# Half-chunk products in column halves, scores that alternate heads, and earlier loads, in a four-mixer decoder layer

## The chip, the cores and the metric

The kernel runs on one core of one Trainium2 chip. Its time is what the device takes for one execution, in microseconds (us). TensorE (PE) multiplies matrices into PSUM banks; VectorE (DVE), ScalarE (ACT) and GpSimd (POOL) work on tiles; the queues of SyncE (SP), ScalarE and GpSimd issue the transfers (DMA). Every engine works through its own instructions in their order, and semaphores let one wait for another.

## The reference

One decoder layer on 1024 tokens of width 1024, all in float32 (`DEPTH` is 1):

```
x = x + 0.5 * swiglu_ffn(rms_norm(x, norm_ffn1), ffn1_w_in, ffn1_w_out)
x = x + token_mixer(rms_norm(x, norm_mix), w_in, w_out, ...)
x = x + 0.5 * swiglu_ffn(rms_norm(x, norm_ffn2), ffn2_w_in, ffn2_w_out)
return rms_norm(x, norm_final)
```

`swiglu_ffn` is `(silu(gate) * up) @ w_out` with `gate, up = split(x @ w_in)` of 2816 columns each. `token_mixer` projects its input and gives four groups of 256 channels to four causal mixers: a pooling over trailing windows; two gated linear attentions (HGRN2 and GLA), each with 4 heads of 64 channels and

```
S_t = diag(a_t) S_{t-1} + k_t^T v_t,    o_t = q_t S_t
```

and RWKV7, a delta rule with 4 heads of 64:

```
S_t = S_{t-1} diag(w_t) - (S_{t-1} kk_t)(kk_t * a_t)^T + v_t k_t^T,    o_t = S_t r_t
```

The four results are normalised, gated and joined, and `w_out` brings them back to 1024 channels.

## The kernel before

**Large products.** An activation or weight tile is split into a high and a low part of type fp32r (`split`, `wload`: ScalarE copies the high part, VectorE subtracts it for the low one), and a product is three fp32r products, high by high, high by low and low by high (`acc3`). Everything goes through the helper on line 89, so in the profile nearly all matmuls carry that line, and the tile names tell them apart. Small products are plain fp32; each leaves two records in the trace.

**The feed-forward blocks** work on pairs of 128-row blocks of the 2816 hidden rows, with seven block products in place of eight (`seven`, `out_seven`). One pair, number `PLAIN` = 0, goes through in the plain way: its four h tiles (two row blocks by two token halves) are written to DRAM (`put_h`, h1d and h2d), and after `out_seven` the four are loaded again, split, and multiplied with their two rows of the output weights. `out_seven` runs over five blocks of pairs, and over four quarters `q` of the output columns in each; in quarter `q` it fetches the weights of the next quarter (`wfetch`, tile wraw, two buffers), prepares those of this one in whi and wlo (four buffers each), and adds seven products into the tiles of x (gr, gg) with VectorE (L672) and GpSimd (L675). In the first block (`ffn1_out`) the plain pair's loop also adds to x (L747) and splits the result for the mixers (`norm_tile`, L177 to L181); its weights go through wraw, whi and wlo by `wload`. In the second (`ffn2_out`) the loop works on token-major tiles (`token_major`, L794, L796), and the final norm follows.

**The mixers** (`weave`) are one stream of large products (`dense_stream`) into which the steps of several generators are put: `rwkv` (delta rule), `gates` (the two attentions) and others. A generator yields a time from the table `LAT`; a clock that counts the estimated cost of each matmul decides when its next step is due, and the order of TensorE's instructions is fixed by it. The list that Tile schedules gives these steps priority over the dense stream.

**The attentions** (`attend`, called for two mixers, two channel pairs and two token halves, 8 times). A tile holds two heads by 512 tokens, in four columns of 128 tokens. The decays within a chunk of 128 are handled by seven levels of block size m = 1, 2, 4, 8, 16, 32, 64: at a level, the odd blocks' queries of both heads are put block-diagonally into `bdt`, k by `bdt` gives the scores of that level in a bank pg, and for m < 64 a mask copy (L1547, `copy_predicated`) puts the right ones into `PT`, whose entries hold scores of 128 keys by 128 queries per column and head. For m < 64 the keys and queries that count lie in the same half of 64 tokens; rows 64 to 127 by columns 0 to 63 of `PT` stay zero. At the end, for each of the four columns, one product of q with the state `Sb` and one product of `PT` with the values `Vp` per head go into the bank O.

**The delta rule** (`rwkv_unit`, 4 units of two heads by 8 chunks of 64). Its scores are 16 products, each of the 64 rows of one head (rows 0 to 63 or 64 to 127), into banks px of four chunks; VectorE multiplies each bank with two masks (L1293, L1294). The inverse and the chunk recurrence (banks py and po) follow.

## Time and profile before

| | us |
|---|---|
| median of 3 runs | 2066.91 |
| lowest, highest | 2062.92, 2071.9 |
| the profiled execution | 2059.14 |
| its span, first to last instruction | 2057.3 |
| PE busy in it | 1979.4 (96%) |
| DVE busy | 1541.1 (75%) |
| ACT busy | 964.2 (47%) |
| POOL busy | 442.0 (21%) |

The profile is of one execution. A row of the timeline gives the start and the length of a run of like instructions, the engine, the line, the operation, the tiles written and read, the tile shape for a matmul (rows by columns of the array, then partitions by columns of the moving operand), and in brackets the idle time before it and what ended that. Matmuls are pipelined, so lengths overlap, and starts are the safer reading. PEld is the load of the stationary operand, SPq a DMA issue of SyncE's queue. A row of the waits gives who waited for whom: us in total, times, longest. A row of the groups gives busy us, mean ns of one, and idle time before them.

### The profile page before, as it was taken

The page shows a single profiled execution, that of the slowest core. Times are in us where ns is not written, and L with a number is a line of the kernel's source. Part 1 is how long each engine was busy: PE and PEld are TensorE (multiplying, and loading weights), DVE is VectorE, ACT ScalarE, POOL GpSimd, SP SyncE. Part 2 cuts the span into 40 slices and gives each one's busy share as a digit, 9 for nine tenths or more (in the row PEclk, how much of TensorE's full clock was granted, in tenths as well). Part 3 has the DMA queues.
Part 4 walks back from the last instruction along what each step waited for, and adds up shares of the span by engine and source line. Part 5 has one row for each costly group of instructions (what it writes and reads, how often), then busy time and mean ns, then how long its engine had stood idle before and what let it go on. Part 6 is the DMA issues. An engine that isn't in the chain of part 4 may idle for free. (4 is left out here: it accounts for less than half of the span.)

```text
span 2057.3 us, 29356 instructions
## 1 busy us (share of the span) xinstructions
PE 1979.4 (96%) x10424; PEld 1594.1 (77%) x10424; DVE 1541.1 (75%) x2575; ACT 964.2 (47%) x1801; POOL 442.0 (21%) x449
## 2 busy tenths in 40 slices
PE   7899999999999899989999999999999999999995
PEld 5688888887887678778778787787888887778884
DVE  5868878768878856486576676676978898777786
ACT  7435444544443655343464543444544444444444
POOL 0011110003446602002020010100111222134464
PEclk9999999999999999999999999999999999999998
DMA  8336554457653453333443244655445666786622
GB/s 275 114 93 205 200 189 161 157 186 280 253 203 138 156 159 108 91 92 97 145 147 106 83 140 134 207 172 160 139 162 187 202 211 215 242 289 254 246 89 91
DMA packets 304402, 348.60 MB, mean 169 GB/s; under 512 B 28160, under 2 KB 230240, under 8 KB 304256
## 3 DMA queue, kind: packets, MB, share of 16 engines
q1 hardware_dynamic: 301152, 339.14, 49.8%
q0 software_dynamic: 1664, 4.95, 0.7%
q10 hardware_dynamic: 1440, 2.65, 0.4%
q8 instruction: 82, 1.34, 0.3%
q14 instruction: 64, 0.52, 0.1%
HBM read 234.22 MB, written 112.46 MB: 169 GB/s over the span
## 5 line engine op out<-in xcount | busy, mean ns | idle before, releaser
L89 PE MATMUL mm<-xs,whi 128*128 128x512 f32 x1568 | 521.0, 413 | 10.3 <-ACT xs L177 3.9
L89 PEld LDWEIGHTS mm<-xs,whi 128*128 128x128 f32 x1568 | 287.4, 192 | 81.5 <-issue 8.5
L89 PE MATMUL mm<-xs,wlo 128*128 128x512 f32 x784 | 315.4, 402 | 12.1 <-DVE wlo L146 9.7
L145 ACT CAST whi<-wraw 128x512 fp32r<-128x512 f32 (+1 forms) x192 | 118.1, 620 | 171.7 <-PE mm L89 121.1
L300 ACT CAST whi<-wsum 128x512 fp32r<-128x512 f32 x176 | 108.3, 620 | 179.2 <-PE pq L89 49.4
L89 PEld LDWEIGHTS mm<-xs,wlo 128*128 128x128 f32 x784 | 150.6, 192 | 50.4 <-DVE wlo L146 12.1
L89 PE MATMUL pq<-xs,whi 128*128 128x512 f32 x576 | 181.0, 394 | 2.3 <-ACT xs L177 1.8
L146 DVE TENSOR_TENSOR wlo<-wraw,whi 128x512 fp32r<-128x512 f32 (+1 forms) x192 | 134.3, 707 | 63.2 <-ACT whi L145 51.1
L89 PE MATMUL pg<-xs,whi 128*128 128x512 f32 x560 | 176.9, 395 | 4.7 <-DVE hx L559 2.7
L89 PE MATMUL px<-xs,whi 128*128 128x512 f32 x560 | 175.2, 393 | 1.2 <-DVE xs L178 1.2
L301 DVE TENSOR_TENSOR wlo<-wsum,whi 128x512 fp32r<-128x512 f32 x176 | 121.5, 697 | 28.2 <-ACT whi L300 27.9
L89 PE MATMUL pq<-xe,whi 128*128 128x512 f32 x448 | 139.2, 392 | 0.0
L89 PEld LDWEIGHTS pq<-xs,whi 128*128 128x128 f32 x576 | 108.5, 189 | 27.2 <-ACT xs L177 2.7
L89 PEld LDWEIGHTS pg<-xs,whi 128*128 128x128 f32 x560 | 105.0, 189 | 29.5 <-issue 3.1
L89 PEld LDWEIGHTS px<-xs,whi 128*128 128x128 f32 x560 | 105.2, 188 | 25.9 <-DVE xs L178 2.3
L89 PE MATMUL pq<-xs,wlo 128*128 128x512 f32 x288 | 114.2, 396 | 3.8 <-DVE wlo L301 3.8
L340 POOL TENSOR_TENSOR tmp<-tmp 128x512 f32<-128x512 f32 x22 | 33.1, 1503 | 374.0 <-ACT tmp L330 310.6
L89 PE MATMUL pg<-xs,wlo 128*128 128x512 f32 x280 | 110.3, 394 | 0.0
L89 PE MATMUL px<-xs,wlo 128*128 128x512 f32 x280 | 109.9, 392 | 0.0
L89 PEld LDWEIGHTS pq<-xe,whi 128*128 128x128 f32 x448 | 84.3, 188 | 18.7
L622 ACT CAST whi<-wsum 128x512 fp32r<-128x512 f32 x80 | 49.7, 621 | 95.1 <-PE px L89 25.5
L340 POOL TENSOR_TENSOR gr<-gr 128x512 f32<-128x512 f32 x18 | 36.6, 2031 | 256.7 <-ACT gr L330 198.0
(460 smaller groups left out, 4319.9 us busy)
## 6 DMA issues: line engine op xcount, KB each, us to landing
hs<-hx SPq DMA_DIRECT2D x126, 512.0 KB, 3.4
xs<-hs SPq DMA_DIRECT2D x90, 512.0 KB, 6.5
wraw<-in_ffn_w_in SPq DMA_DIRECT2D x68, 512.0 KB, 4.1
wraw<-in_w_in SPq DMA_DIRECT2D x52, 512.0 KB, 4.1
wrawb<-in_ffn_w_in SPq DMA_DIRECT2D x44, 512.0 KB, 4.6
wraw<-in_ffn_w_out SPq DMA_DIRECT2D x42, 512.0 KB, 3.6
xe<-hs SPq DMA_DIRECT2D x36, 512.0 KB, 7.4
wraw<-in_w_out SPq DMA_DIRECT2D x16, 512.0 KB, 4.1
```

The source lines that it names most:

```text
L89: return self._add(self.nc.tensor.matmul(out, lhsT=lhsT, rhs=rhs, **kw), n * 0.42e-3 if rhs.dtype == F32R else max(n * 1.68e-3, 0.04))
L145: nc.scalar.copy(hi[:, :n], raw[:, sl])
L146: nc.vector.tensor_tensor(lo[:, :n], raw[:, sl], hi[:, :n].bitcast(F32), op=ALU.subtract)
L300: nc.scalar.copy(hi[:, :H], a)
L301: nc.vector.tensor_tensor(lo[:, :H], a, hi[:, :H].bitcast(F32), op=ALU.subtract)
L340: nc.gpsimd.tensor_tensor(kept[5], kept[5], kept[7], op=ALU.add)
L622: nc.scalar.copy(v(hi), src)
```

## The change

There are three parts.

*Loads.* `out_seven` gets an argument `late`, a function that it calls in the last block when quarter q = 2 begins, after the fetch of quarter 3. In `ffn1_out` it loads and splits the plain pair's four h tiles and its four weight tiles, the latter through `tmp` into tiles hx and xe instead of wraw, whi and wlo. In `ffn2_out` it loads the final norm's gain and loads and splits the four h tiles; the weights stay where they were.

```
+                if last and q == 2:
+                    late()
...
+        def late():
+            hs.extend([[h_tile(f, h) for h in range(2)] for f in (f0, f0 + 1)])
+            for n in range(0, KT, 2):
+                raw = wk.tile([P, H], F32, name="tmp")
+                nc.sync.dma_start(raw.rearrange("p (f c) -> p f c", c=256), wo[:, f0:f0 + 2, n * P:(n + 2) * P])
+                if n < 6:
+                    t = wk.tile([P, 2 * H], F32R, name="hx", bufs=3)
+                else:
+                    t = wk.tile([P, 2 * H], F32R, name="xe", bufs=6)
+                hi, lo = self.split(raw, t=t)
+                w.append([(hi[:, f * 256:f * 256 + 256], lo[:, f * 256:f * 256 + 256]) for f in range(2)])
...
-        hs = [[h_tile(f, h) for h in range(2)] for f in (f0, f0 + 1)]
-        w = [self.wload([(wo[:, f0:f0 + 2, n * P:(n + 2) * P], 0, None)], 2, 256, 1) for n in range(0, KT, 2)]
...
+        def late():
+            gf = self.gf = wk.tile([P, D], F32, name="wrawb", bufs=2)
+            nc.scalar.dma_start(gf, self.A["norm_final"].broadcast_to([P, D]))
+            for f in (f0, f0 + 1):
+                hp.append([])
+                for h in range(2):
+                    t = tmp()
+                    nc.sync.dma_start(t, self.hd[f, h])
+                    hp[-1].append(self.split(t))
```

*Scores of the delta rule.* The same 16 products come in two halves of four chunks; in a half, the products of the two heads alternate and go into two banks. One yield of twice the time stands where two stood.

```
-        for c2 in range(4):
-            ps = self.px.tile([P, 4, P], F32, name="px")
-            hd = c2 // 2
-            hs = slice(hd * 64, hd * 64 + 64)
+        for half in range(2):
+            banks = [self.px.tile([P, 4, P], F32, name="px") for _ in range(2)]
             for i in range(4):
...
+                for hd, ps in enumerate(banks):
+                    hs = slice(hd * 64, hd * 64 + 64)
+                    te.matmul(ps[:, i], lhsT=bk[hs, 4 * half + i].rearrange("p x t -> p (x t)"),
+                              rhs=rK[hs, 4 * half + i].rearrange("p x t -> p (x t)"), start=True, stop=True)
...
-            if c2 in (1, 2):
-                yield LAT["score"]
+            if half == 0:
+                yield 2 * LAT["score"]
```

*The attentions.* At a level with m < 64 each half of 64 tokens has a product of its own (64 keys by 32 queries of each head), into the output partitions of its half; the mask copy becomes two of 64 partitions. The product of `PT` with the values becomes two: queries 0 to 63 with keys 0 to 63, and queries 64 to 127 with all 128 keys, each into the output partitions of its queries.

```
-                te.matmul(ps[:, j].rearrange("p x t -> p (x t)"), lhsT=k[:, j * P:(j + 1) * P],
-                          rhs=self.bdt[:, i % 2, j].rearrange("p x t -> p (x t)"), start=True, stop=True)
+                if m < 64:
+                    for u in range(2):
+                        te.matmul(ps[u * 64:u * 64 + 64, j, :, 0:32], lhsT=k[:, j * P + u * 64:j * P + u * 64 + 64],
+                                  rhs=self.bdt[:, i % 2, j, :, u * 32:u * 32 + 32], start=True, stop=True)
...
+                for u in range(2):
+                    us, n = slice(u * 64, u * 64 + 64), 32 // m
+                    dst = PT.rearrange("p j x (n y m) -> p (j x) n y m", y=2, m=m)[us, :, u * n:u * n + n, 1]
+                    msk = self.gmask[us, 64 * i + u * 32:64 * i + u * 32 + 32].rearrange("p (n m) -> p n m", m=m)
+                    nc.vector.copy_predicated(dst, msk.unsqueeze(1).broadcast_to([64, 8, n, m]), ...)
...
-                te.matmul(O[:, j, hs], lhsT=PT[:, j, hd], rhs=Vp[:, j, hs], start=False, stop=True,
-                          skip_group_check=True)
+                for u in range(2):
+                    r = slice(0, 64 * u + 64)
+                    te.matmul(O[u * 64:u * 64 + 64, j, hs], lhsT=PT[r, j, hd, u * 64:u * 64 + 64], rhs=Vp[r, j, hs],
+                              start=False, stop=True, skip_group_check=True)
```

## The prediction

> **What bounds the kernel now.** I read the page first: TensorE is busy for 96% of the span and VectorE for 75%, so whatever takes TensorE time out of the middle of the program should show one for one, and only where TensorE idles can another engine set the pace. The stretches of 50 us and the waits then say where it idles.

> ```profile
> span 2057.3 us, 29356 instructions
> PE 1979.4 (96%) x10424; PEld 1594.1 (77%) x10424; DVE 1541.1 (75%) x2575; ACT 964.2 (47%) x1801; POOL 442.0 (21%) x449
> ...
> 650.00:700.00 50.00, 38.67 (x159) 29.04 (x158) 48.68 (x58) 29.94 (x51) 36.67 (x25) 0.96 0.41 148
> ...
> PE mm L89 <- DVE wlo L146: 9.7, 4, 7.0
> ...
> PE pg L89 <- DVE PT L1547: 6.4, 1, 6.4
> ```

> The columns after the stretch are its length, then PE, PEld, DVE, ACT, POOL, clock, DMA share and GB/s. Two of the three things edited lie in the mixers (about 700 to 1320 us), where TensorE waits little except once for 6.4 us on PT; the third lies at the two ends of the feed-forward blocks, of which the first, 650 to 700, has 11.3 us without a matmul while VectorE is busy for 48.7 of 50. For the mixers I therefore read single matmul groups on the timeline: an occupancy is the start of a group to the start of what follows it. An fp32 product leaves two records in the trace, an fp32r product one.

> **The attention levels.** Eight attentions have six levels each that change: 4 products of a 128x128 tile (8 records) become 8 of a 128x64 tile with 64 columns (16 records), going by turns to output partitions 0-63 and 64-127. Exactly that form is already in the kernel: the state products of the same attention (pg<-gin,gg).

> ```profile
> 779.85 1.05 PE L89 MATMUL pg<-bdt,gin 128*128 128x128 f32 x8
> 780.66 0.37 PE L89 MATMUL mm<-whi,xs 128*128 128x256 f32 x1
> ...
> 793.37 0.28 PE L89 MATMUL mm<-whi,xs 128*128 128x256 f32 x1
> 793.58 0.69 PE L89 MATMUL pg<-gin,gg 128*64 128x64 f32 x16
> 794.20 0.39 PE L89 MATMUL mm<-whi,xs 128*128 128x256 f32 x1
> ...
> 820.37 1.05 PE L89 MATMUL pg<-bdt,gin 128*128 128x128 f32 x8
> 821.35 0.34 PE L89 MATMUL py<-gr 128*64 128x64 f32 x4
> 821.51 0.40 PE L89 MATMUL po<-gr 128*64 128x64 f32 x4
> 821.84 0.73 PE L89 MATMUL mm<-xs,whi 128*128 128x512 f32 x2
> ```

> A level costs 0.81 us today (779.85 to 780.66). Sixteen records of the new form cost 0.62 (793.58 to 794.20), and the product before them is held to 0.21 where its neighbours of that width take 0.12, so 0.71: 0.10 less, and I take 0.08 for a small loss on the way out. Where a level is followed by products in the 128x64 shape it costs 0.98 now (820.37 to 821.35): 0.17 goes to the change of shape, and after the edit that change is gone or has moved. Going through the timeline, 28 of the 48 levels stand between full-width products (28 x 0.08 = 2.2); 7 touch a group in the same 128x64 shape (about 0.4 each, 2.9) and 13 a group of another small shape (about 0.3 each, 3.9). **Gain 9.0 us.** Bounds: 0 (the new groups land elsewhere and nothing is shared) and 48 x 0.4 = 19.

> The mask copy becomes two on half the partitions each.

> ```profile
> L1547 DVE COPY_PREDICATED PT<-gmask,pg 128x512 f32<-128x512 uint32 x48 | 43.7, 910 | 0.1
> L1294 DVE TENSOR_TENSOR gr<-px,rmask 128x256 f32<-128x256 f32 x16 | 6.6, 413 | 0.0
> ```

> Ninety-six copies of 256 elements at the 413 ns of the nearest row of that size would be 39.7 us against 43.7; at half of today's mean plus 100 ns they would be 53.3. VectorE hides it, so I cost it at 0.5. Without that cover it is the 6.4 us wait above over again, in which a level's products stood behind PT: bounds -1 and +13 (two more such waits).

> **The values product.** Here I see the loss. Per pair of chunks there is one full product with the state (2 records) and two 128x128 products with 64 columns (4 records). After the edit the two become four, by turns 64 rows by 64 columns and 128 rows by 64 columns, so that every product has another tile shape than the one before it, the full one included.

> ```profile
> 798.45 0.44 PE L89 MATMUL pg<-Sb,gin 128*128 128x128 f32 x2
> 798.72 0.56 PE L89 MATMUL pg<-gin,PT 128*128 128x64 f32 x4
> 799.12 0.44 PE L89 MATMUL pg<-Sb,gin 128*128 128x128 f32 x2
> ...
> 753.71 1.09 PE L89 MATMUL px<-sel,t 128*64 128x2 f32 x16
> 754.73 2.05 PE L89 MATMUL px<-gr 64*128 64x128 f32 x16
> ...
> 832.26 0.44 PE L89 MATMUL py<-gr 64*64 64x64 f32 x4
> 832.63 0.32 PE L89 MATMUL po<-sbd,gr 128*64 128x128 f32 x1
> 832.65 0.33 PE L89 MATMUL pg<-gin,gg 128*64 128x64 f32 x2
> ```

> A pair takes 0.67 now (798.45 to 799.12). Four 64x64 records ahead of a change of shape take 0.37 (832.26 to 832.63), though a record in an unbroken run of one shape takes 0.064 (1.02 us for sixteen, 753.71 to 754.73): 0.11 of it is the change. The product after the 64x64 group at 832.63 writes the upper output half, since the group at 832.65, which begins in the lower half, starts 0.02 us after it and runs beside it; so the delay falls also where the two halves don't overlap. Two records and a change of shape are then 0.37 - 2 x 0.064 = 0.24, four such pieces 0.96, and the full product 0.27 (798.45 to 798.72) plus the 0.17 of leaving the full shape, 0.44: 1.40 per pair, 0.73 more. Thirty-two pairs: **loss 23.4 us**, all of it in a queue that hardly idles. Bounds: if the halves ran beside each other as in 821.35 to 821.51 (4 records in 0.16), eight records take 0.32 and the pair 0.76, +2.9 in all; if a piece took the whole 0.37, 1.92 per pair, +40. I stay at 23.4, because the 832 row has the shapes and halves in question.

> [...]

> **The delta rule's scores.** Sixteen products per unit, four units. Neighbours now use different 64 rows of the array. The only pair in the kernel that does that is the two LoRA products.

> ```profile
> 735.34 1.13 PE L89 MATMUL px<-rin,w2a 64*128 64x512 f32 x4
> ...
> 749.50 1.98 PE L89 MATMUL px<-raw,glaw 16*128 16x512 f32 x4
> ...
> 760.47 1.20 PE L89 MATMUL px<-gr 64*128 64x128 f32 x8
> ...
> 763.89 1.16 PE L89 MATMUL px<-gr 64*128 64x128 f32 x8
> ```

> On different rows four records of 512 columns take 1.13, on the same rows 1.98, and their loads are as wide as those of the scores. A unit has 2.05 (754.73) + 1.20 + 1.16 = 4.41 now; with pairs side by side each half of 16 records takes what 8 take, 1.18, so 2.36. **Gain 4 x 2.05 = 8.2 us.** Bounds: with no overlap two groups of 16 are 4.10, gain 1.2; more than half cannot overlap, so 8.8. The one wait of twice the length stands for the two removed. Two banks are asked for at once instead of one; VectorE needs 4 x 0.41 (row L1294) = 1.7 us to free them and the planner puts 3.4 between the halves, so that costs nothing unless VectorE is behind.

> **The loads.** End of the first feed-forward block:

> ```profile
> 641.23 0.67 DVE L623 TENSOR_TENSOR wlo<-wraw,whi 128x512 fp32r<-128x512 f32 x1
> 643.49 1.10 DVE L631 TENSOR_TENSOR wsum<-wraw 128x256 f32<-128x256 f32 x1 [1.59 <-DMA wraw<-in_ffn_w_out]
> ...
> 651.18 10.51 SPq L137 DMA_DIRECT2D wraw<-in_ffn_w_out  x3
> 661.80 1.83 SPq L732 DMA_DIRECT2D tmp<-h1d  x4
> ...
> 666.40 0.50 PE L89 MATMUL mm<-xs,whi 128*128 128x512 f32 x1 [2.81 <-ACT xs L177]
> ...
> 682.11 0.60 ACT L145 CAST whi<-wraw 128x512 fp32r<-128x512 f32 x1
> ...
> 698.70 2.36 DVE L146 TENSOR_TENSOR wlo<-wraw,whi 128x512 fp32r<-128x512 f32 x2
> ...
> 699.44 0.79 PE L89 MATMUL mm<-xs,wlo 128*128 128x512 f32 x1 [7.00 <-DVE wlo L146]
> ```

> The four h loads stand in SP's queue behind weight loads that wait for a wraw buffer, and land late: 2.81 us. VectorE, busy for 48.7 of the 50 us from 650 on, has the mixers' first weights last in its queue: 7.00 us. The edit moves 8 loads (2 MB) and the 8 ScalarE and 8 VectorE halves of their splits ahead of the last two quarters. SP reaches the loads behind the quarter's own fetch; the transfers have room (DMA share 0.41), and so has ScalarE (29.9 of 50; eight of 0.60). VectorE has none: no work of its own goes, so its chain up to 698.70 can shorten only by gaps such as the 1.59 before 643.49. What does help: the plain pair no longer holds whi, wlo and wraw, so the mixers' first split needn't wait for a release (the first whi runs at 682.11, when the plain pair's weights come free) and can stand ahead of the plain pair's sums. I take the 2.81 as lost again to VectorE and 6 of the 7.00 as won: **gain 6 us.** Bounds: 9.8, both gaps gone; and -3.8, when eight splits of 0.67 (5.4 us) hold up the last quarters' weights and only the gap of 1.59 comes back. Next late after that is VectorE's sum of the plain pair.

> ```profile
> 2008.26 0.66 PE L794 MATMUL px<-ident,gr 128*128 128x128 f32 x4 [1.03 <-ACT xe L796]
> ...
> 2013.64 0.33 PE L794 MATMUL px<-ident,gr 128*128 128x128 f32 x1 [0.92 <-DVE gr L675]
> ```

> At the end of the second block only the four h tiles and the norm's gain (one load on ScalarE's queue) move; the weights stay. Of these two waits I take 1 of 1.95 us. **Gain 1 us**, bounds +2 and -2.

> **Sum** against the profiled execution's 2059.14 (1.84 outside its span of 2057.3): -9.0 + 0.5 + 23.4 - 8.2 - 6 - 1 = -0.3, no change. The median of the three runs is 2066.91, 7.8 above that execution, and I put the forecast on it: 2067. From 0.5% (10 us) on a measurement of this kernel can tell a change.

> **Rivals.** First: the values product's halves do overlap and it costs 2.9. Then the sum is -0.3 - 20.5, 2046, faster. For it speaks that each half owns its output partitions; against it the 832 row. 15%. [...] Second, on the other side: VectorE becomes what the products wait for. Its doubled mask copies and two-bank evacuations stand behind a unit's preparation, and TensorE, in order, waits at the next level. It needs the copies to be later than the planner's 1 us per level; one such wait is 6.4, two more are +13: 2080. The loads gaining nothing on top (+7) would be 2074 by itself, still within 10. 17%. Third: the loads and the levels give their upper bounds (-3.8 and -10): 2053. For it speaks that 20 levels already touch small shapes; 8%. The forecast keeps 60%, its own range 2057 to 2077.

> **Numbers.** Faster: 15 and 8, less a little that ends within 0.5%, 0.22. Slower: 17 and some of the forecast's upper tail, less those waits that stay under 10 us, 0.20. The same: 0.58. The range takes in the first rival and the second one: 2043 to 2082.

> **What would show it.** Levels: 16 records in the 128x64 shape in about 0.62. Values: pg<-gin,PT in the shapes 64x64 and 128x64, 1.4 us from one Sb group to the next; 0.76 proves the first rival. Scores: 16 records in 1.2. Loads: tmp<-h1d issued near 641, no 7 us wait at L146 after the plain pair. Wrong: PE waits on PT or gr in the mixers by more than 10 us in all.

## The result, and the profile after

The changed kernel takes 2127.23 us (median of 4 runs, 2123.62 to 2131.15) against 2066.19 for the kernel before (4 runs): 1.0293 times, 95% interval 1.0259 to 1.0327. It is slower by 61 us, well outside the predicted range of 2043 to 2082. The profiled executions, 2123.73 and 2059.14, differ by 64.6 us.

The row of the clock that was granted to TensorE, on the page of the kernel before:

```profile
PEclk9999999999999999999999999999999999999998
```

The page of the changed kernel:

```profile
span 2122.0 us, 30419 instructions
PE 2027.8 (96%) x10936; PEld 1606.6 (76%) x10936; DVE 1552.2 (73%) x2623; ACT 965.3 (45%) x1801; POOL 440.0 (21%) x449
...
PEclk9999999999999997989998997999999999999998
```

TensorE is 96% busy as before, with 48 us more busy time. The clock row had only nines before, up to the last slice; now it has sevens and eights in the middle. The same in stretches; first the kernel before, then the changed one (length, then PE, PEld, DVE, ACT, POOL, clock, DMA share, GB/s):

```profile
700.00:900.00 200.00, 190.11 (x1355) 154.89 (x1354) 121.73 (x260) 98.21 (x197) 31.86 (x69) 0.97 0.39 113
900.00:1100.00 200.00, 198.57 (x1496) 158.14 (x1494) 133.53 (x276) 94.72 (x191) 28.02 (x73) 0.95 0.45 131
1100.00:1300.00 200.00, 198.22 (x1532) 157.04 (x1532) 134.97 (x287) 89.68 (x196) 18.47 (x41) 0.99 0.40 120
```

```profile
700.00:900.00 200.00, 188.18 (x1384) 146.86 (x1382) 105.48 (x232) 89.19 (x177) 31.72 (x70) 0.89 0.37 108
900.00:1100.00 200.00, 183.22 (x1362) 137.07 (x1362) 131.91 (x276) 91.31 (x179) 16.30 (x42) 0.92 0.38 110
1100.00:1300.00 200.00, 194.50 (x1686) 148.69 (x1684) 132.31 (x286) 83.05 (x180) 25.95 (x66) 0.90 0.34 101
```

The reader should look at the clock column: 0.97, 0.95, 0.99 became 0.89, 0.92, 0.90. In the records the granted clock is always 1.0 or 0.5, in pieces whose length is a multiple of 3.41 us (but for the last of a run, which the end cuts off). I add up those pieces over the whole span, and TensorE's idle time:

| whole span, us | before | after | difference |
|---|---|---|---|
| length | 2057.3 | 2122.0 | +64.6 |
| time at half clock (half of it is counted as lost) | 71.3 | 163.8 | +46.2 lost |
| TensorE idle | 78.0 | 94.2 | +16.2 |
| the rest: work at full clock | 1943.7 | 1945.9 | +2.2 |

The split is rough: in the changed kernel at half clock records of 512 columns start 0.43 us apart (815.21 to 816.06, two of them) for 0.23 at full clock, and a pair of the values product takes 2.35 us for 1.42 (rows below), so each loses less than half its speed; and the clock's records begin 14 to 20 us after the span does (what lies ahead of them is counted at full clock, in every kernel alike). `loads_only` below, with the same products as the kernel before, comes out 2.3 us lower in the last row, so differences of that size say nothing. Nearly all of the loss lies in the mixers: they begin 2.6 us later (the last write to DRAM ahead of them is issued by 700.5 instead of 697.9), last 782.7 us instead of 720.9 up to the end of their last sum, and what follows takes 0.3 us more. So the work came out about even, and nearly all of the loss is clock and waits.

### The profile page after: what moved, and what is told of

It is laid out like the page before. It is cut to its first block, busy times and chain, and to the rows that moved or that the text cites. A ratio compares the mean times of both kernels' runs of the same rounds, so it can differ in the third digit from the quotient of the medians.

```text
span 2122.0 us, 30419 instructions
## 1 busy us (share of the span) xinstructions
PE 2027.8 (96%) x10936; PEld 1606.6 (76%) x10936; DVE 1552.2 (73%) x2623; ACT 965.3 (45%) x1801; POOL 440.0 (21%) x449
## 3 DMA queue, kind: packets, MB, share of 16 engines
q8 instruction: 86, 1.41, 0.3%
## 5 line engine op out<-in xcount | busy, mean ns | idle before, releaser
L89 PE MATMUL mm<-xs,whi 128*128 128x512 f32 x1536 | 522.4, 422 | 10.8 <-DVE st L1153 4.6
L89 PEld LDWEIGHTS mm<-xs,whi 128*128 128x128 f32 x1536 | 288.3, 197 | 82.3 <-issue 12.2
L89 PE MATMUL mm<-xs,wlo 128*128 128x512 f32 x768 | 314.7, 410 | 5.1 <-DVE wlo L146 2.7
L145 ACT CAST whi<-wraw 128x512 fp32r<-128x512 f32 (+1 forms) x188 | 115.7, 620 | 176.4 <-PE mm L89 128.0
L300 ACT CAST whi<-wsum 128x512 fp32r<-128x512 f32 x176 | 108.3, 620 | 177.6 <-PE pq L89 52.8
L89 PEld LDWEIGHTS mm<-xs,wlo 128*128 128x128 f32 x768 | 151.4, 197 | 44.3 <-DVE wlo L623 4.7
L89 PE MATMUL pq<-xs,whi 128*128 128x512 f32 x576 | 180.7, 393 | 2.3 <-ACT xs L177 1.8
L146 DVE TENSOR_TENSOR wlo<-wraw,whi 128x512 fp32r<-128x512 f32 (+1 forms) x188 | 131.2, 706 | 66.8 <-ACT whi L145 57.8
L89 PE MATMUL px<-xs,whi 128*128 128x512 f32 x560 | 175.3, 393 | 2.2 <-DVE xs L178 1.2
L89 PE MATMUL pg<-xs,whi 128*128 128x512 f32 x528 | 167.3, 397 | 3.4 <-DVE hx L559 2.7
L89 PE MATMUL pq<-xe,whi 128*128 128x512 f32 x448 | 139.2, 392 | 0.0
L89 PEld LDWEIGHTS pq<-xs,whi 128*128 128x128 f32 x576 | 108.5, 189 | 27.2 <-ACT xs L177 2.7
L89 PEld LDWEIGHTS px<-xs,whi 128*128 128x128 f32 x560 | 105.1, 188 | 27.3 <-DVE xs L178 2.3
L89 PE MATMUL pq<-xs,wlo 128*128 128x512 f32 x288 | 114.4, 397 | 8.8 <-DVE wlo L623 4.8
L89 PEld LDWEIGHTS pg<-xs,whi 128*128 128x128 f32 x528 | 99.8, 190 | 26.6 <-issue 3.1
L89 PE MATMUL px<-xs,wlo 128*128 128x512 f32 x280 | 109.9, 392 | 0.0
L89 PE MATMUL pg<-xs,wlo 128*128 128x512 f32 x264 | 104.6, 396 | 0.0
L89 PEld LDWEIGHTS pq<-xe,whi 128*128 128x128 f32 x448 | 84.3, 188 | 18.8
L340 POOL TENSOR_TENSOR gr<-gr 128x512 f32<-128x512 f32 x18 | 37.2, 2066 | 256.9 <-ACT gr L330 179.3
```

The lines of the kernel that those rows point to most:

```text
L89: return self._add(self.nc.tensor.matmul(out, lhsT=lhsT, rhs=rhs, **kw), n * 0.42e-3 if rhs.dtype == F32R else max(n * 1.68e-3, 0.04))
L145: nc.scalar.copy(hi[:, :n], raw[:, sl])
L146: nc.vector.tensor_tensor(lo[:, :n], raw[:, sl], hi[:, :n].bitcast(F32), op=ALU.subtract)
L300: nc.scalar.copy(hi[:, :H], a)
L340: nc.gpsimd.tensor_tensor(kept[5], kept[5], kept[7], op=ALU.add)
```

## The terms of the sum in the trace after

Values product, at full clock and in another attention at half clock:

```profile
801.70 0.39 PE L89 MATMUL pg<-Sb,gin 128*128 128x128 f32 x2
802.02 1.10 PE L89 MATMUL pg<-gin,PT 64*64 64x64 f32 x8
803.04 0.49 PE L89 MATMUL pg<-Sb,gin 128*128 128x128 f32 x2
...
807.38 0.90 PE L96 MATMUL px<-ident,gr 16*16 16x16 f32 x32
...
1138.41 0.80 PE L89 MATMUL pg<-Sb,gin 128*128 128x128 f32 x2
1139.14 1.68 PE L89 MATMUL pg<-gin,PT 64*64 64x64 f32 x8
1140.76 0.80 PE L89 MATMUL pg<-Sb,gin 128*128 128x128 f32 x2
```

(The row names its first shape, 64x64; half of its 8 records are 128x64.) The rows from 801 on are at full clock, those from 1138 at half. From 801.70 to 807.38 an attention takes 5.68 us, 1.42 per pair; forecast 1.40. Before it was 2.72, so at full clock the edit costs 8 x 2.96 = 23.7 us, for 23.4 forecast. At half clock a pair takes 2.35. Levels and scores, on TensorE:

```profile
756.59 0.48 PE L89 MATMUL px<-gr 64*128 64x128 f32 x2
757.43 1.16 PE L89 MATMUL px<-gr 64*128 64x128 f32 x14 [0.35 <-DVE n L1294]
758.51 0.74 PE L89 MATMUL mm<-xs,whi 128*128 128x512 f32 x2
...
781.24 0.69 PE L89 MATMUL pg<-bdt,gin 128*64 128x64 f32 x16
781.86 0.74 PE L89 MATMUL mm<-xs,whi 128*128 128x512 f32 x2
...
926.15 1.48 PE L89 MATMUL px<-gr 64*128 64x128 f32 x16
927.56 1.16 PE L89 MATMUL pg<-bdt,gin 128*128 128x128 f32 x8
...
932.21 1.16 PE L89 MATMUL px<-gr 64*128 64x128 f32 x16
933.30 0.69 PE L89 MATMUL pg<-gin,gg 128*64 128x64 f32 x16
```

A level of 16 records takes 0.62 (forecast 0.62). A half of the scores takes 1.41 and 1.09 in the second unit (forecast 1.18 each), but 1.92 and 1.72 in the first, where the products stop after the first two records: the other head's bank is not free until VectorE has read what stood in it (n, L1294, whose 0.16 us begin at 757.21; in the unit's other half a mask, L1311). The eight halves, one of them partly at half clock, take 11.6 us, where the four units took 16.7 before: 5.1 less, for 8.2 forecast. So the values and the levels do what the forecast says, the scores in part. What the forecast did not contain is the clock. Five of the clock's 3.41 us windows around the first values product, on the grid of its records:

```profile
797.57:800.98 3.41, 3.41 (x40) 3.21 (x39) 1.92 (x6) 1.54 (x5) 0.00 (x0) 1.00 0.33 82
...
804.39:807.81 3.42, 3.42 (x43) 2.57 (x43) 0.32 (x1) 0.44 (x2) 0.00 (x0) 1.00 0.58 161
807.81:811.22 3.41, 3.41 (x43) 2.61 (x37) 1.56 (x4) 2.80 (x7) 1.17 (x1) 0.50 0.32 114
...
835.12:838.53 3.41, 3.41 (x17) 2.37 (x18) 2.12 (x5) 0.94 (x2) 0.18 (x1) 0.50 0.01 2
838.53:841.94 3.41, 3.30 (x47) 2.30 (x43) 2.83 (x8) 2.44 (x6) 0.00 (x0) 1.00 0.02 5
```

TensorE is busy for all of 804.39 to 807.81, and yet the next window and the eight behind it run at half clock. Being busy is not what counts. I worked out another measure from the matmul records: the time in which columns stream, times the rows and columns of the tile as a share of 128x128, over the window. A column is put at 0.45 ns (fp32r records of 512 columns start 0.23 us apart), in fp32 at twice that (records of 128 columns start 0.112 us apart), and at half clock at twice again, which is rough (0.43 for the 0.23, as above). That share of the array, an estimate, is 0.24 in 804.39 to 807.81 and 0.97 in 835.12 to 838.53, after which the clock returned. Over all windows of the sixteen profiles of this study that the clock's records cover:

| window at full clock, share of the array | windows | next one at half |
|---|---|---|
| under 0.35 | 168 | 156 |
| 0.35 to 0.40 | 63 | 40 |
| 0.40 to 0.45 | 128 | 18 |
| 0.45 and over | 8825 | 0 |

| window at half clock, share of the array | windows | next one still at half |
|---|---|---|
| under 0.70 | 242 | 242 |
| 0.70 to 0.80 | 17 | 12 |
| 0.80 and over | 196 | 3 |

In 70 of the 130 halvings in the mixers TensorE had been busy for 98% or more of the window before. Of all windows at full clock in which it was that busy, 60 of the 89 with a share under 0.40 were followed by half clock, and none of the 8168 with 0.45 and over. The weight by rows and columns is needed: without it windows up to 0.90 were followed by half clock, and 1903 below that were not; with it the figures are 0.44 and 127. By this measure the edit is expensive exactly where it saves: a pair of the values product streams (0.224 + 2 x 0.115)/0.67 = 0.68 of the array before, and (0.224 + 0.172)/1.42 = 0.28 after, both estimates by the columns, where 0.172 is two products of 0.115 us on a quarter of the array and two on half of it.

## The experiments

The last three columns come from the profiled execution, over the whole span, as in the table above. The mean clock is that of the timed runs. The ratio is to the kernel before as timed beside each.

| kernel | median us | ratio to before, 95% | mean clock | at half clock | idle | work |
|---|---|---|---|---|---|---|
| before | 2063 to 2066 | | 0.979 | 71.3 | 78.0 | 1943.7 |
| after | 2127.23 | 1.0259 to 1.0327 | 0.958 | 163.8 | 94.2 | 1945.9 |
| values_only | 2110.80 | 1.0185 to 1.0284 | 0.967 | 129.5 | 82.9 | 1961.6 |
| levels_only | 2072.55 | 1.0031 to 1.0082 | 0.973 | 93.1 | 86.5 | 1932.4 |
| scores_only | 2082.11 | 1.0054 to 1.0109 | 0.975 | 107.3 | 94.0 | 1935.3 |
| loads_only | 2069.81 | 0.9986 to 1.0030 | 0.978 | 106.8 | 77.9 | 1941.4 |
| pad_dense | 2081.86 | 1.0070 to 1.0108 | 0.984 | 65.5 | 83.3 | 1964.4 |
| pad_narrow | 2119.88 | 1.0201 to 1.0297 | 0.963 | 177.6 | 82.8 | 1956.6 |
| values_fill | 2112.15 | 1.0186 to 1.0245 | 0.981 | 91.8 | 82.5 | 1985.0 |
| values_cols | 2056.20 | 0.9950 to 0.9982 | 0.981 | 92.0 | 81.5 | 1932.1 |
| values_grouped | 2071.86 | 1.0023 to 1.0055 | 0.977 | 88.7 | 80.8 | 1945.6 |
| cols_j | 2057.12 | 0.9942 to 0.9974 | 0.980 | 92.4 | 81.2 | 1934.2 |
| scores_clk | 2070.42 | 1.0002 to 1.0032 | 0.977 | 86.3 | 87.1 | 1933.0 |
| cols_scores | 2060.23 | 0.9959 to 0.9995 | 0.980 | 71.6 | 85.3 | 1931.5 |
| cols_levels | 2071.35 | 1.0007 to 1.0047 | 0.973 | 113.1 | 87.9 | 1922.5 |
| loads_no_lo | 2056.96 | 0.9937 to 0.9982 | 0.981 | 86.2 | 70.5 | 1943.4 |

**One part at a time.** The first four are the kernel before with one hunk of the diff each.

values_only:

> The kernel before with the values product alone edited. Theory (clock): the four chains of 64x64 and 128x64 products between full ones take 0.73 us more per pair (23 us in 32 pairs), and because the array is idle through much of each chain the clock is granted at half for longer: most of the added 92 us at half clock (165.6 after, 73.2 before) come back here, worth half their length, 30 to 46 us. Time 2110 to 2135. Rival A (changes of shape alone): +23 and the clock as before, 2090. Rival B (the time is the loads' or the levels'): within 10 us of the kernel before.

2110.80 us, +46: the low end of what the clock theory gave. In the profiles 18 us of the loss is work and 5 idle time; in the timed runs the clock falls from 0.979 to 0.967, worth about 27 us of the 2110.

levels_only:

> The kernel before with the attention levels alone edited (products in column halves and two mask copies). The clock theory says the clock stays as before, since the groups get shorter and have no chain of shape changes: gain 9 us, 2058. Rival: the 16 narrow records also read as an idle array, the half-clock time grows by 20 us or more: 2068 or more.

Miss for the theory's first form, which had the clock unchanged. The work falls by 11.3 us, more than forecast, but the time rises by 8: the half-clock time by 22 us in the profile (clock 0.973 in ten runs), idle by 8.5. By the same estimate a level now streams half of what it did (8 x 0.115 x 0.5 = 0.46 us of full array, for 0.92), but takes 0.65 us for 0.90 (means at full clock, by the starts), so the share falls.

scores_only:

> The kernel before with the delta rule's scores alone edited. Prediction's term: -8.2 us, 2058, clock as before. The trace after shows the alternating 16 records in 1.8 to 2.0 us and not in 1.2 where they stand alone, so the halves overlap only in part: gain nearer 2 to 4 us, 2063. Rival (the two banks asked for at once make products wait): 2068 or more.

Slower by 17 us, on the rival's side, although the work falls by 8.4: idle rises by 16 and the half-clock time by 36 us in the profile.

loads_only:

> The kernel before with the moved loads alone, at both ends. The trace after has the 7.00 us wait at L146 gone, but 4.76, 2.85 and 2.34 us in new places close by, and the mixers start 2.5 us late: time 2066 to 2071, the clock as before. Rival (the prediction's term): -7, 2059.

No difference that can be told (0.9986 to 1.0030), as expected from the trace after. The single profile has more half-clock time than the mean of its runs.

**Is it the share of the array?** Two kernels make TensorE longer by the same amount in the same place of the kernel before, with full tiles only; they differ in the width of what is added. (At full clock the records of both kinds start 0.11 us apart: 8 in 0.89 us, 968.85 to 969.74 in pad_dense and 976.88 to 977.77 in pad_narrow.)

```
# pad_dense
-            te.matmul(O[:, j], lhsT=q[:, j * P:(j + 1) * P], rhs=self.Sb[:, j], start=True, stop=True)
+            for _ in range(4):
+                te.matmul(O[:, j], lhsT=q[:, j * P:(j + 1) * P], rhs=self.Sb[:, j], start=True, stop=True)
# pad_narrow
+            for _ in range(3):
+                te.matmul(O[:, j, 0:2], lhsT=q[:, j * P:(j + 1) * P], rhs=self.Sb[:, j, 0:2], start=True, stop=True)
+                te.clk += 0.175
```

pad_dense:

> The kernel before with each of the 32 full products of the values with the state (128x128) issued four times over instead of once; the last three only repeat it. TensorE gets about as much longer as by the values edit: 32 x 3 x 0.224 us = 21.5 us. Theory (the clock follows the share of the array that streams in a window of 3.41 us, weighted by the rows and columns of each tile; it halves below about 0.4): the added work fills the whole array, so the clock stays at or above 0.979: 2086 us. Rival (anything that lengthens this chain, or shifts the plan, brings the half clock): clock 0.97 or less as in values_only, 2105 or more.

pad_narrow:

> The counterpart of pad_dense: three more products per pair, of the same 128x128 tile and in the same place of the plan, but 2 columns wide instead of 128. The products of that form (px<-sel,gg) start 0.112 us apart, as the full ones do, so TensorE gets longer by the same 32 x 3 x 0.224 = 21.5 us, with no change of tile shape anywhere. The share of the array in a pair falls from 0.68 to 0.454/1.34 = 0.34, below the 0.39 under which windows halved the clock. Theory (share of the array): clock 0.965 to 0.974, 2095 to 2115. Rival (changes of tile shape, or small tiles, bring the half clock): clock as pad_dense, 0.98 or more, 2080 to 2087.

The narrow padding costs 57 us (2119.88 against 2063.11 of the kernel before on the same chip), 5 more than the upper end of what was expected, and the dense one 18 (2081.86 against 2064.01). The rows of 1100 to 1300, first pad_dense, then pad_narrow:

```profile
1100.00:1300.00 200.00, 196.98 (x1686) 161.94 (x1685) 124.51 (x267) 83.83 (x184) 17.30 (x38) 0.97 0.36 104
```

```profile
1100.00:1300.00 200.00, 196.93 (x1394) 162.92 (x1394) 115.91 (x248) 76.74 (x167) 22.74 (x59) 0.84 0.32 91
```

TensorE is busy for 197 of 200 us in both; the clock is 0.97 and 0.84. Neither has a new change of shape, so those are not needed for it. That the clock follows how much streams, and not how busy TensorE is, is shown. That the rows and columns of a tile count as well rests on the counts over the windows alone.

values_fill is values_only with the loop of pad_dense:

> values_only with the same three repeats of the full product in each pair. The share of the array in a pair rises from (0.224 + 0.172)/1.40 = 0.28 to (0.896 + 0.172)/2.07 = 0.52. Theory: 21.5 us more work, but the clock goes back from 0.968 to about 0.979, which returns about 23 us: 2105 to 2115, no slower than values_only in spite of the work. Rival (the narrow products themselves bring the half clock, whatever runs beside them): 2130 or more, clock 0.968.

2112.15 against 2110.80: 32 x 3 products more, and no time lost by it (work +23, half-clock time 129.5 to 91.8). The narrow products stayed; dense work among them brought the clock back to 0.981.

**The values product in other forms.**

```
# values_cols; cols_j has one loop over j, with the second loop's body in the first
         for j in range(4):
+            for u in range(2):
+                us = slice(u * 64, u * 64 + 64)
+                te.matmul(O[us, j], lhsT=q[:, j * P + u * 64:j * P + u * 64 + 64], rhs=self.Sb[:, j], start=True, stop=True)
+        for j in range(4):
             for hd in range(2):
...
+                for u in range(2):
+                    us = slice(u * 64, u * 64 + 64)
+                    te.matmul(O[us, j, hs], lhsT=PT[:, j, hd, us], rhs=Vp[:, j, hs], start=False, stop=True, ...)
```

values_cols:

> The kernel before with the values product in two column halves throughout: the state product as two 128x64 tiles per pair, the values as 128x64 tiles with all 128 rows (zero rows included), halves by turns, four pairs together, so no change of shape inside. By the state products in 128x64 (16 records in 0.62) an attention takes 8 x 0.112 + 16 x 0.058 + 0.4 = 2.2 us for 2.68 alone: 4 to 7 us less work, array share 0.8. Theory: clock 0.979 or above, 2058 to 2061. Rival (small tiles of any order halve the clock): clock 0.972 or less, 2072 or more.

values_grouped has the four tiles of values_only, in the order Sb for all pairs, then 64x64, then 128x64:

> The kernel before with the products of values_only (the same tiles, counts and columns), but ordered by shape within an attention: four full ones, eight of 64x64, eight of 128x64. The changes of shape fall from 19 to 3, so the work is about 4 x 0.224 + 16 x 0.064 x 2 + 0.43 = 3.4 us per attention (values_only 5.8, before 2.7): +5.5 us, and the array share 0.47. Theory: clock close to before (0.976 to 0.980), 2070 to 2078. Rival (narrow tiles themselves, not the changes of shape): as values_only, 2100 or more.

cols_j:

> values_cols with the products of one pair kept together (two state products, then the four of the values), so that each pair's sum is formed before the next pair starts; same tiles and counts, no change of shape inside. [...] Theory: the order inside one shape costs nothing, 1.95 us per attention as there (2.68 before): 2056 to 2059, clock 0.979 to 0.983. Rival (the turn from 128-column to 64-column products costs something each time): up to 0.1 us for each of 32 pairs, 2062.

With the same small tiles in an order with 3 changes of shape in place of 19, most of the 46 us goes: an attention's values take 3.13 us in values_grouped (5.68 in the changed kernel), the clock is 0.977. In one shape throughout it is 1.96, less than the 2.72 of the kernel before; from cols_j:

```profile
801.46 0.44 PE L89 MATMUL pg<-Sb,gin 128*64 128x128 f32 x4
801.73 0.40 PE L89 MATMUL pg<-gin,PT 128*64 128x64 f32 x8
801.96 0.39 PE L89 MATMUL pg<-Sb,gin 128*64 128x128 f32 x4
...
803.42 0.87 PE L96 MATMUL px<-ident,gr 16*16 16x16 f32 x32
```

Eight records of the values take 0.23 (801.73 to 801.96), 0.029 each, where a record of this tile shape takes 0.064 in the unbroken run at 753.71 of the kernel before: inside one shape the halves do run beside each other. cols_j beats both kernels, 2057.12 us, 0.4% under the kernel before. In values_cols and values_grouped the starts of later pairs come between the state product and the values of an earlier one, and, as I read it, their sums leave out the state part of three pairs, which no run shows by itself; as the instructions are the same, the time is read as it is.

**Where the gain of the scores went.**

```
# scores_clk: scores_only, and
+            te.clk -= 0.6
             for hd, ps in enumerate(banks):
                 ss = slice(8 * hd + 4 * half, 8 * hd + 4 * half + 4)
```

> scores_only, with 0.6 us per half taken off the planner's charge for the scores (it charges 1.72 us for a half that now takes 1.1 to 1.4). Theory: scores_only is slow because the plan runs ahead of the chip by 1 us and more per unit, so products come due before their operands (idle 37 us in the mixers for 22 before) and those idle windows halve the clock; with the charge mended the waits fall to 25 us or less and the gain of 7 to 9 us shows: 2058 to 2065. Rival (two banks asked for at once, and the masks bunched behind one wait, are what makes products wait): idle stays above 33 us, 2078 or more.

Half right: idle falls from 94.0 to 87.1 and the time by 12 us, to 2070.42, but 9 us of idle more than before remain. (The expectation counts idle time in the mixers, with the whole of the 7.00 us wait at their start: 22 before, 37 in scores_only, and 29 here.) The largest of it, PE's row first, then VectorE's:

```profile
1051.85 1.13 PE L89 MATMUL mm<-xs,whi 128*128 128x512 f32 x2 [4.63 <-DVE st L1137]
```

```profile
1049.09 0.69 DVE L178 TENSOR_TENSOR xs<-st,xs 128x512 fp32r<-128x512 f32 x1 [1.49 <-ACT xs L177]
1049.70 0.41 DVE L1295 TENSOR_TENSOR gr<-px,rmask 128x256 f32<-128x256 f32 x1
...
1050.70 0.41 DVE L1296 TENSOR_TENSOR gr<-px,rmask 128x256 f32<-128x256 f32 x1
1051.03 1.27 DVE L1137 TENSOR_TENSOR st<-mm,rsb 128x512 f32<-128x512 f32 x2
```

VectorE waits for ScalarE, then does the four masks of both banks in one go, and only then takes the dense product's bank, for which TensorE waits. In the kernel before the wait for this tile is 0.51 us, since TensorE still has scores to do then. This is the rival's mechanism, and it accounts for 4.1 of the 9 us; where the others come from was not followed up.

cols_scores:

> cols_j and scores_clk together. Theory: the two gains add: 2050 to 2056. Rival as in scores_clk: 2072 or more.

2060.23, above the 2050 to 2056 expected. The two changes do add (cols_j 8.7 us below the kernel before, scores_clk 3.5 above it, both together 4.7 below), but the second is no gain. For cols_levels:

> cols_j and the attention levels as edited. Theory: the levels save 11 us of work but halve the array work in a time that hardly changes (0.46 for 0.92 us of full array in 0.82 for 0.90 us), which lowers the share and costs the clock 6 to 9 us and the waits 9: no gain over cols_j, 2058 to 2068. Rival (with the values dense there is room for the lower share): 2050.

No gain over cols_j, as the theory has it: work 1922.5, the least of all, and a clock of 0.973. But 2071.35 lies 3 us above its range.

**The loads.** loads_no_lo is loads_only with the low halves of the eight early splits left out.

```
     # split(), called with low=False by late() and its h_tile
             nc.scalar.copy(hi, src)
+            if not low:
+                return hi, hi
             nc.vector.tensor_tensor(lo, src, hi.bitcast(F32), op=ALU.subtract)
```

> loads_only, in which the eight splits moved ahead at the end of the first block leave out their low halves on VectorE (the high half stands in for the low one, so the plain pair is computed to less precision); 8 x 0.60 = 4.8 us of VectorE work goes, every load, ScalarE cast and product stays. Theory (VectorE's chain bounds this stretch: 58.9 of 62 us busy from 640 to 702 in loads_only as in before, and the wait only moved): TensorE's waits from 630 to 715 fall from 10.0 us to 5 to 6 and the last of the stretch's spills starts at 696 instead of 701; time 3 to 5 us below loads_only. Rival (the transfers or their place in SP's queue bound it): the waits and the time stay within 1 us.

TensorE's waits in this stretch, loads_only first, then loads_no_lo:

```profile
PE pq L89 <- DVE wlo L623: 5.5, 1, 5.5
PE px L89 <- POOL o L212: 2.9, 1, 2.9
PE px L89 <- POOL rstok L227: 0.9, 1, 0.9
```

```profile
PE px L89 <- POOL o L214: 2.9, 1, 2.9
```

Its idle time from 630 to 715 falls from 10.0 to 3.7 us, more than the 4 to 5 expected, and the ratio to the kernel before is 0.9960 (0.9937 to 0.9982) where loads_only has 1.0008 (0.9986 to 1.0030): some 10 us, for 3 to 5 expected, of which the waits are 6.4. VectorE's chain is the bound there, not the transfers.

## Why the prediction was wrong

By its own steps:

- **Values product**: right in size (1.40 forecast, 1.42 per pair; 23.4 and 23.7 us), and the first rival is out. Its price in time was 46 us (values_only), about 27 of them by the clock, because the stretched chain brings the half clock. What the row at 832 and the rows at 821 showed holds each in its place: the changes of shape cost (5.68 us with them, 3.13 with most of them gone), and inside one shape the tiles run beside each other (0.23 us for eight records in cols_j).
- **Levels**: 0.62 us as forecast, 11.3 us less work for 9.0 forecast. The clock and 8.5 us of new waits turned that into +8. In the changed kernel the 96 mask copies take 51.2 us, 533 ns each, 78 over half of the 910 before; the 100 ns of the forecast's upper figure was an estimate that no row showed. Whether the doubled mask copies brought the waits, against the step "VectorE hides it", or the shorter groups, was not separated.
- **Scores**: the groups got 5.1 us shorter, for 8.2 forecast. The step that failed is "costs nothing unless VectorE is behind": VectorE was behind (the second bank of the halves of 1.92 and 1.72 us waits for it), and the planner charges 1.72 us for a half that takes 1.1 to 1.4 where it doesn't wait, so later products came due too early. Alone this part made the kernel 17 us slower.
- **Loads**: the 7.00 us wait at L146 went, as the prediction said it would. That 6 us of it would be won did not follow. The changed kernel's rows:

```profile
657.98 0.80 PE L89 MATMUL pq<-xs,wlo 128*128 128x512 f32 x1 [4.76 <-DVE wlo L623]
703.19 1.05 PE L89 MATMUL px<-ones,o 128*128 128x1 f32 x8 [2.85 <-POOL o L212]
707.39 2.08 PE L89 MATMUL px<-ident,rstok 128*128 128x128 f32 x8 [2.34 <-POOL rstok L227]
```

  The prediction itself had said that VectorE's chain "can shorten only by gaps such as the 1.59", and should have gone by it.
- **The sum**: -0.3 forecast. Of it, +6.2 is work on TensorE (levels, values and scores); the work rose by 2.2 us, which the rough split can't tell from it. The step that failed is above all of them: every duration was taken from rows at full clock, and the clock was treated as given. The column was in the quoted row of 650 to 700 (0.96) and was not used. 46 of the 64.6 us are there, and 16 more are waits, where the sum had 6.5 us fewer. The sign named for a wrong forecast, waits on PT or gr of over 10 us, did not come up (PT 7.5, gr 0.7); the clock was not among the signs. The second rival, VectorE as what the products wait for, named a part of it, but at 2080 in all.

What stays open: at which share exactly the clock halves (between 0.35 and 0.45 some windows do and some don't), and how much of the waits in the changed kernel would go at full clock.

## What to carry to other kernels

Read the granted clock beside the busy share, stage by stage, before pricing an edit: an edit that takes more work off the array than time off TensorE can lose its gain to the clock, as levels_only did (11.3 us less work, 22 us more at half clock, 8 us slower). Work out, for each group, how much of the array streams in a window of the clock (3.41 us here): by the estimate above, none of the windows of 0.45 and over was followed by half clock, and of those under 0.35 156 of 168 were. Here small products among dense ones went with a higher clock (values_fill 0.981, values_only 0.967), and so did neighbours of the same tile shape (cols_j 0.980): a product in halves made this kernel 0.4% faster in one shape (cols_j) and in changing shapes 2.4% slower (values_only). When a wait is removed from a chain on another engine, ask how long that chain is, not how long the wait.
